# A hybrid state-space and attention layer: branch products over all tokens in three parts, an ungated first half, and fewer VectorE operations

## The chip, the core and the metric

The kernel runs on one core of a Trainium2 chip. The metric is the device time of one execution in microseconds (us); the kernel before takes 2579.67 us in the median of 3 runs (2579.16 to 2581.6). The core's engines run side by side, each through its own list of instructions in order: TensorE (PE; its weight loads are listed apart as PEld), VectorE (DVE), ScalarE (ACT), GpSimd (POOL) and SyncE (SP), which issues all DMAs of this kernel. Engines wait for one another by semaphores. Matrix products go to PSUM, everything else lies in SBUF, and large intermediate arrays go to scratch arrays in DRAM.

## The reference, cut to what matters

One layer is applied to 1024 tokens of a prompt and to 64 tokens of a running stream with caches. With xn = RMSNorm(x), one projection gives z, xBC, dt, q, k, v and two gates. Then:

```
proj = xn @ w_in
z, xbc, dt_raw, q, k, v, gate_ssm, gate_att = split(proj)
xbc_c = silu(causal_dwconv(xbc))                        # -> xs, bm, cm
y_ssm, ssm_new = ssd_scan(xs, softplus(dt_raw + bias), a_neg, bm, cm, ssm_past, 64)
y_ssm = group_rmsnorm((y_ssm + ssm_d * xs) * silu(z)) * ssm_norm_w
o = rmsnorm(diff_attention(rope(norm(q)), rope(norm(k)), v, lam)) * subln_w * (1 - lambda_init)
mix = sigmoid(gate_ssm) * (y_ssm @ w_branch_ssm) + sigmoid(gate_att) * (o @ w_branch_attn)
x = x + mix @ w_out
h = rmsnorm(x) @ w_up;  ha, hb = halves of h
x = x + (silu(causal_dwconv(ha)) * hb) @ w_down
```

`w_branch_ssm` has 2048 rows and 1024 columns, `w_branch_attn` and `w_out` 1024 by 1024. Everything is float32.

## The kernel before, in words

All activations lie transposed: 128 features on the partitions, the 1088 tokens (1024 + 64) along the free axis. `WIDE` cuts the tokens into 384, 384 and 320. Every large product is made in three passes for float32 accuracy: `weights` (line 125) loads a block of a weight matrix, rounds it into `w_hi` on ACT (line 136) and leaves the remainder `w_lo` on VectorE (line 137); `product` (line 140) issues hi*hi, hi*lo and lo*hi for each of 8 blocks of 128 rows, 24 matmuls into one PSUM tile. The pool `wp` has two sets of weight buffers; the PSUM pool `pm` has two tiles, handed out by `acc`.

The stages in order:

- Norm of the input in chunks of `NORM` tokens (lines 238 to 261). It writes `xn_hi` and `xn_lo`, two tiles of 8 x 1088 columns, on which all projections run. `rstd_of` (line 209) makes 1/sqrt(mean + eps) from a logarithm, an exponential and one Newton step, four VectorE operations.
- `values`, `heads` for q and k, `steps` for dt. `steps` also writes the running sums of dt*a to `a_sc` and their exponentials to `e_sc`, both in DRAM.
- Attention by heads (line 616). The remaining projections are a stream of tiles, `ORDER` (line 67): z, convolved xBC ("c") and gates ("g"), each block of 128 features in three parts of tokens. `fill(rate)` takes `rate` tiles of that stream after each piece of work, `ATT_STEPS` in attention and `SCAN_STEPS` in the scan. The gates are kept as tanh(g/2), so that sigmoid(g) is (1 + tanh)/2, and the half is put into the output projection (line 805).
- The scan, `scan` (line 731): 4 groups of heads by 3 spans of tokens, each span of three steps of 128 tokens (`step`, line 658) and a closing `gated` (line 714). A step loads running sums as `bc`, to all partitions (line 663), and their exponentials as `e2` (line 668); `bc` is masked on POOL (line 682), goes through eight exponentials on ACT (line 684) and a multiply on VectorE (line 685), and is the operand of the products `yi`. Products `ye` with the state are scaled by `e2` (line 697). `fetch` loads the next span, `gate` applies silu to it on ACT, with the change of the activation table that this needs. `gated` normalizes and writes `y_sc`.
- The branch products, `branch` (line 156), three times: the attention output (`o_sc`, with its gate, to `m_sc`), the first half of the scan's channels (`y_sc[:D]`, gate and `m_sc` added, to `n_sc`), the second half (`y_sc[D:]`, gate and `n_sc` added, split into `mix`). Tokens are cut into two halves of 544; for each half, 8 blocks of output rows; for each block the weights are loaded and split again, and two products of 272 columns made. VectorE empties PSUM with the gating multiply (line 196) and adds the earlier branch (line 198). Rows of `y_sc` come through staging tiles `b_f` (three buffers) and are split on ACT and VectorE (lines 167 to 170); rows of `o_sc` were stored split and are loaded directly. Their pool `br` takes the place of `xn_pool` after that is released.
- The first two branches are the tail of the stream: from scan span `BRANCH_AT` on, `fill` takes tiles of `branch_tiles` (line 756). What is left runs after the scan, then the third branch (line 784), then the output projection with the second norm (line 793) and the feed-forward part (line 826).

The order on each engine comes from a planner, not from the text alone: it walks a timeline of expected durations, and of the instructions that are then ready it takes those that stand first in the text, moved up by `tc.high_priority(ahead)`. A branch tile can therefore be issued earlier than its place in the text where TensorE would be free. `issue_after` pins an instruction behind another. Pools that are released and reallocated make the new tiles wait for the last use of the old ones.

Of the kernel before, what the change touches and what calls it, by code (L numbers as in the profile page):

```python
# [31 lines left out]
NORM = (128, 256, 256, 256, 192)  # L32
# [10 lines left out]
BG = 4  # L43
LAG = 2
# [13 lines left out]
SCAN_STEPS = 2.5  # L58
SPLIT = 5
BRANCH_AT = 9  # L60


def group(g):
# [4 lines left out]
         ("z", range(4, 8)), ("c", group(3)), ("z", range(8, 16)))  # L68
# [8 lines left out]
def hybrid_layer(ctx: ExitStack, tc: tile.TileContext, xT, prm, cst, rope, wvd, win, wbs, wba, wout, wup, wdn,  # L77
# [18 lines left out]
    a_sc, e_sc = scratch("a_sc", [32, T]), scratch("e_sc", [32, T])  # L96
# [24 lines left out]
    xn_hi = xn_pool.tile([P, KT, T], R32, name="xn_hi")  # L121
    xn_lo = xn_pool.tile([P, KT, T], R32, name="xn_lo")
# [24 lines left out]
    def project(block, evac):  # L147
        w_hi, w_lo = weights(block, KT, P)
        for c, w in WIDE:
            ps = acc(w)  # L150
            product(ps, [(w_hi[:, k], w_lo[:, k], xn_hi[:, k, c : c + w], xn_lo[:, k, c : c + w]) for k in range(KT)])
            with tc.high_priority(quick or ahead):
                evac(ps, c, w)
            yield

    def branch(stage, pair, src, wts, g0, add, out):
        def octet():
            return [br.tile([P, 8, HALF], R32, name=n, tag=n, bufs=2) for n in ("b_hi", "b_lo")]

        def bring(c, k, hi, lo):  # L160
            if stage is None:
                for u, t in enumerate((hi, lo)):
                    load(out=t[:, k].bitcast(F32), in_=src[D * u + P * k : D * u + P * (k + 1), c : c + HALF])
                return
            for a in (0, HALF // 2):
                q = slice(a, a + HALF // 2)
                t = stage()
                load(out=t, in_=src[P * k : P * (k + 1), c + a : c + a + HALF // 2])
                S.copy(hi[:, k, q], t)
                V.tensor_tensor(out=lo[:, k, q], in0=t, in1=hi[:, k, q], op=ALU.subtract)  # L170

        parts = [octet(), None]
        for k in range(8):
            bring(0, k, *parts[0])
        for x, c in enumerate((0, HALF)):
            hi, lo = parts[x]
            if x == 0:
                parts[1] = octet()
            for m in range(KT):
                r = slice(P * m, P * (m + 1))  # L180
                two = pair()
                gt, at = two[:, :HALF], two[:, HALF:T]
# [809 lines left out]
```

## Time and profile before

| what | value |
|---|---|
| median of 3 runs | 2579.67 us |
| profiled execution, its own time | 2582.58 us |
| span of that execution, first to last instruction | 2580.8 us |
| mean granted TensorE clock | 0.995 |
| TensorE idle time in the span | 55.8 us (2580.8 - 2525.0) |
| scan with projection tiles | 1097 to 1262 us |
| scan with branch products | 1262 to 1592 us |
| third branch | 1592 to 1691 us |
| output projection and second norm | 1691 to 1802 us |

A stretch of the span is described by one line of the window view: its borders and length in us, then for each engine the busy us and, in brackets, the number of instructions, then the granted TensorE clock (1.00 is full), the share of time in which the 16 DMA engines were busy, and GB/s. A line of the view of waits reads: engine and line that waited, what ended the wait, total us, number of times, longest. A line of the group view reads: line, engine, operation, output<-inputs, sizes, count | busy us, mean ns of one | idle us of the engine just before them, and what ended it. Matmuls overlap in the pipeline, so the spacing of their starts, not the duration listed, is what one costs.

### The profile page before, as it was taken

The numbers are of one execution on the slowest core, as the hardware profiler recorded it, in microseconds if no ns is written. First come the engines' busy times: TensorE is split into PE (matmuls) and PEld (weight loads), VectorE is DVE, ScalarE is ACT, GpSimd is POOL, SyncE is SP. The second block draws the span as 40 slices with busy tenths as digits, with TensorE's granted clock in tenths as the row PEclk, the third lists the DMA queues.
The fourth block names the chain that finished last, engine by engine and source line by source line (L and its number), as shares of the span: only waits on it lengthen the run. The fifth ranks groups of instructions, "written<-read, shape, count | busy, mean of one in ns | idle before, by whom it ended". The sixth has DMA issues, their size and how long they took to land.

```text
span 2580.8 us, 41810 instructions
## 1 busy us (share of the span) xinstructions
PE 2525.0 (98%) x16484; PEld 2444.8 (95%) x16484; DVE 1399.8 (54%) x2371; ACT 1032.2 (40%) x2113; POOL 290.0 (11%) x387
## 2 busy tenths in 40 slices
PE   8999999999999999999999989999999999999999
PEld 7999999999999999988788879999999999999999
DVE  7326266654447674665679997658333333343333
ACT  5334234544445554565456643335312222131221
POOL 3000001000001110022333430023000000000000
PEclk9999999999999999999999999999999999999999
DMA  5217167545435433176798978555311111111112
GB/s 162 83 54 282 51 257 213 153 142 148 131 126 164 136 112 111 64 232 192 245 332 258 304 246 272 195 187 193 119 42 47 44 42 50 42 50 40 44 43 77
DMA packets 233685, 366.59 MB, mean 142 GB/s; under 512 B 31184, under 2 KB 160464, under 8 KB 233360
## 3 DMA queue, kind: packets, MB, share of 16 engines
q1 hardware_dynamic: 233488, 363.91, 44.2%
q8 instruction: 130, 2.13, 0.3%
q14 instruction: 67, 0.55, 0.1%
HBM read 263.56 MB, written 100.27 MB: 141 GB/s over the span
## 4 chain that ended last, share of the span: by engine, by line
PE 43%; DMA 3%; DVE 3%; ACT 1%; issue 1%; SPq 0%; POOL 0%; DVEq 0%; ACTq 0%; POOLq 0%
PE mm L143 7%; PE mm L145 7%; PE mm L144 7%; PE up L143 7%; PE up L145 7%; PE up L144 7%; DMA in<-x_sc 1%; DMA b_hi<-o_sc 1%; DVE w_lo L137 1%; PE yi L689 1%; PE stp L702 0%; ACT bc L684 0%; DVE y L728 0%; DMA in<-z_sc 0%; DVE b_lo L170 0%
## 5 line engine op out<-in xcount | busy, mean ns | idle before, releaser
L143 PE MATMUL mm<-xn_hi,w_hi 128*128 128x320 f32 (+1 forms) x1496 | 497.9, 333 | 2.3 <-ACT zr L428 1.1
L145 PE MATMUL mm<-xn_hi,w_lo 128*128 128x320 f32 (+1 forms) x1496 | 496.8, 332 | 0.0
L144 PE MATMUL mm<-xn_lo,w_hi 128*128 128x320 f32 (+1 forms) x1496 | 494.6, 331 | 0.0
L136 ACT CAST w_hi<-w_f 128x1024 fp32r<-128x1024 f32 (+2 forms) x220 | 229.3, 1042 | 547.2 <-PE mm L144 369.3
L137 DVE TENSOR_TENSOR w_lo<-w_f,w_hi 128x1024 fp32r<-128x1024 f32 (+2 forms) x220 | 284.9, 1295 | 300.8 <-ACT w_hi L136 298.4
L143 PE MATMUL up<-x_hi,w_hi 128*128 128x384 f32 (+1 forms) x1056 | 345.0, 327 | 2.7 <-ACT x_hi L820 2.7
L144 PE MATMUL up<-x_lo,w_hi 128*128 128x384 f32 (+1 forms) x1056 | 344.8, 327 | 0.0
L145 PE MATMUL up<-x_hi,w_lo 128*128 128x384 f32 (+1 forms) x1056 | 343.3, 327 | 0.0
L143 PEld LDWEIGHTS mm<-xn_hi,w_hi 128*128 128x128 f32 x1496 | 281.9, 188 | 7.9 <-issue 2.8
L145 PEld LDWEIGHTS mm<-xn_hi,w_lo 128*128 128x128 f32 x1496 | 281.6, 188 | 2.9 <-issue 1.9
L144 PEld LDWEIGHTS mm<-xn_lo,w_hi 128*128 128x128 f32 x1496 | 281.8, 188 | 2.6 <-issue 1.3
L143 PE MATMUL mm<-b_hi,w_hi 128*128 128x272 f32 x768 | 228.0, 298 | 19.1 <-DVE b_g L196 15.9
L144 PE MATMUL mm<-b_lo,w_hi 128*128 128x272 f32 x768 | 227.2, 296 | 0.7 <-DMA b_lo<-o_sc 0.7
L145 PE MATMUL mm<-b_hi,w_lo 128*128 128x272 f32 x768 | 227.5, 297 | 0.0
L143 PEld LDWEIGHTS up<-x_hi,w_hi 128*128 128x128 f32 x1056 | 198.7, 188 | 3.1 <-ACT x_hi L820 3.0
L144 PEld LDWEIGHTS up<-x_lo,w_hi 128*128 128x128 f32 x1056 | 198.8, 188 | 0.1
L145 PEld LDWEIGHTS up<-x_hi,w_lo 128*128 128x128 f32 x1056 | 198.5, 188 | 0.0
L880 DVE TENSOR_TENSOR xa<-xa,mm 128x384 f32<-128x384 f32 x144 | 76.5, 531 | 197.3 <-PE mm L145 197.3
L144 PE MATMUL mm<-f_lo,w_hi 128*128 128x384 f32 (+1 forms) x528 | 173.1, 328 | 0.0
L143 PE MATMUL mm<-f_hi,w_hi 128*128 128x384 f32 (+1 forms) x528 | 173.0, 328 | 0.0
L145 PE MATMUL mm<-f_hi,w_lo 128*128 128x384 f32 (+1 forms) x528 | 173.0, 328 | 0.0
L143 PEld LDWEIGHTS mm<-b_hi,w_hi 128*128 128x128 f32 x768 | 147.3, 192 | 25.4 <-DVE b_g L196 15.4
(252 smaller groups left out, 4803.7 us busy)
## 6 DMA issues: line engine op xcount, KB each, us to landing
w_f<-in_win_dram SPq DMA_DIRECT2D x76, 512.0 KB, 4.0
w_f<-in_wup_dram SPq DMA_DIRECT2D x44, 512.0 KB, 3.7
bc<-a_sc SPq DMA_DIRECT2D x32, 512.0 KB, 6.3
w_f<-in_wbs_dram SPq DMA_DIRECT2D x32, 512.0 KB, 4.2
b_g<-g_sc SPq DMA_DIRECT2D x48, 272.0 KB, 4.5
w_f<-in_wout_dram SPq DMA_DIRECT2D x24, 512.0 KB, 3.8
x_sc<-cc SPq DMA_DIRECT2D x48, 192.0 KB, 1.9
kh_t<-k_st SPq DMA_DIRECT2D x32, 272.0 KB, 6.9
```

The costliest lines, as they stand in the source:

```text
L136: S.copy(hi, w)
L137: V.tensor_tensor(out=lo, in0=w, in1=hi, op=ALU.subtract)
L143: PE.matmul(ps, a_hi, b_hi, start=i == 0, stop=False)
L144: PE.matmul(ps, a_hi, b_lo, start=False, stop=False)
L145: PE.matmul(ps, a_lo, b_hi, start=False, stop=i == n - 1)
L689: PE.matmul(yi[u : u + 64, e // 2, :L], xdt[:L, e], bc[:L, e, :L], start=True, stop=True)
L880: V.tensor_tensor(out=xa[:, m, c : c + w], in0=xa[:, m, c : c + w], in1=ps, op=ALU.add)
```

## The change

- `branch` runs over all 1088 tokens: for a turn of one or two blocks of output rows (`TURNS`) it loads and splits the weights once and then makes products of 384, 384 and 320 columns for the three parts of `WIDE`. One call yields 24 tiles instead of 16 larger ones.
- Projection rows and branch rows are kept as three pairs of tiles, one per part of `WIDE`, and the branch rows use the same tags of `xn_pool`: each part takes the place of the earlier part as soon as that has had its last use. The last two z blocks run part by part in alternation.
- The second branch is stored without gate and sum (ACT copies it out of PSUM). The third branch adds it to its own product, gates the sum once, and adds the attention branch: three VectorE operations a tile.
- `SCAN_STEPS` 2.5 becomes 1.65 and `BRANCH_AT` 9 becomes 4; side tiles `b_g` become eight of 384 columns instead of four of 1088.
- The exponentials `e2` are made in the step by two ACT instructions from `bc`, ahead of the mask; `e_sc` goes.
- The two multiplies with dt in the step become one with a broadcast operand.
- `rstd_of` gives the negative root with one more ACT square and two VectorE operations instead of four; the norm weights in `par` are negated once to make up for it.
- `NORM` has six chunks instead of five, with borders on those of `WIDE`.

```diff
-NORM = (128, 256, 256, 256, 192)
+NORM = (128, 256, 192, 192, 192, 128)
-BG = 4
-LAG = 2
+BG = 8
+TURNS = ((0, 1), (2,), (3,), (4,), (5,), (6, 7))
-SCAN_STEPS = 2.5
+SCAN_STEPS = 1.65
-BRANCH_AT = 9
+BRANCH_AT = 4
-         ("z", range(4, 8)), ("c", group(3)), ("z", range(8, 16)))
+         ("z", range(4, 8)), ("c", group(3)), ("z", range(8, 14)))
+    def rows_by_part(name):
+        return [[xn_pool.tile([P, KT, w], R32, name=f"{name}_{u}{x}", tag=f"{u}{x}") for u in ("hi", "lo")]
+                for x, (c, w) in enumerate(WIDE)]
+    xn = rows_by_part("xn")
...
+    def branch(stage, side, src, wts, gates, adds, out):
+        parts = rows_by_part("b")
+        for (c, w), (hi, lo) in zip(WIDE, parts):
+            for k in range(8):
+                if stage is None:
+                    for u, t in enumerate((hi, lo)):
+                        load(out=t[:, k].bitcast(F32), in_=src[D * u + P * k : D * u + P * (k + 1), c : c + w])
+                else:
+                    t = stage()[:, :w]
+                    load(out=t, in_=src[P * k : P * (k + 1), c : c + w])
+                    S.copy(hi[:, k], t)
+                    V.tensor_tensor(out=lo[:, k], in0=t, in1=hi[:, k], op=ALU.subtract)
+        for ms in TURNS:
+            wt = [weights(wts[m], KT, P) for m in ms]
+            for (c, w), (hi, lo) in zip(WIDE, parts):
+                for m, (w_hi, w_lo) in zip(ms, wt):
+                    beside = []
+                    for d, r0 in ([(g_sc, gates)] if gates is not None else []) + [(d, 0) for d in adds]:
+                        t = side()[:, :w]
+                        load(out=t, in_=d[r0 + P * m : r0 + P * (m + 1), c : c + w])
+                        beside.append(t)
+                    to = beside[0] if beside else side()[:, :w]
+                    ps = acc(w)
+                    product(ps, [(w_hi[:, k], w_lo[:, k], hi[:, k], lo[:, k]) for k in range(KT)])
                     with tc.high_priority(ahead):
+                        if not beside:
+                            S.copy(to, ps)
+                        elif not adds:
+                            V.scalar_tensor_tensor(to, to, 1.0, ps, ALU.add, ALU.mult)
+                        else:
+                            V.tensor_tensor(out=beside[1], in0=beside[1], in1=ps, op=ALU.add)
+                    if adds:
+                        V.scalar_tensor_tensor(to, to, 1.0, beside[1], ALU.add, ALU.mult)
+                        V.tensor_tensor(out=to, in0=to, in1=beside[2], op=ALU.add)
+                    out(m, c, to)
+                    yield
...
         act(r, u, AF.Exp, scale=-0.5)
-        V.tensor_scalar(u, mean, -0.5 * scale, -0.5 * EPS, ALU.mult, ALU.add)
-        V.tensor_tensor(out=u, in0=u, in1=r, op=ALU.mult)
-        V.tensor_tensor(out=u, in0=u, in1=r, op=ALU.mult)
-        V.scalar_tensor_tensor(out, u, 1.5, r, ALU.add, ALU.mult)
+        act(u, r, AF.Square, scale=math.sqrt(0.5 * scale))
+        V.scalar_tensor_tensor(u, mean, EPS / scale, u, ALU.add, ALU.mult)
+        V.scalar_tensor_tensor(out, u, -1.5, r, ALU.add, ALU.mult)
...
+                for a, b in ((O_MIX, O_CW), (O_SN, O_D), (O_QN, O_FW)):
+                    V.tensor_scalar_mul(par[:, a:b], par[:, a:b], -1.0)
...
+        two = [z_tiles([j]) for j in (14, 15)]
+        for _ in WIDE:
+            for u in two:
+                yield next(u)
...
-            ev = e_sc.rearrange("(j u) t -> u j t", u=2)
             for u in range(2):
-                src = ev[u, 4 * g : 4 * g + 4, c0 : c0 + L].unsqueeze(0).to_broadcast([64, 4, L])
-                load(out=e2[64 * u : 64 * u + 64, :, :L], in_=src)
+                half = slice(64 * u, 64 * u + 64)
+                act(e2[half, :, :L], bc.rearrange("p (j u) t -> p u j t", u=2)[half, u, :, :L], AF.Exp)
...
-            for dst, sc in ((xdt, dt_tok), (xw, dtw)):
-                V.tensor_tensor(out=dst[:L], in0=tr3, in1=sc[:L, ch, h8].unsqueeze(2).to_broadcast([L, 8, 64]), op=ALU.mult)
+            V.tensor_tensor(out=xx[:L], in0=tr3, in1=dtt[:L, :, ch, h8].unsqueeze(3).to_broadcast([L, 2, 8, 64]), op=ALU.mult)
...
-            yield from branch(None, pair, o_sc, wba, D, None, store(m_sc))
-            yield from branch(stage, pair, y_sc[:D], wbs[0], 0, m_sc, store(n_sc))
+            yield from branch(None, side, o_sc, wba, D, (), store(m_sc))
+            yield from branch(stage, side, y_sc[:D], wbs[0], None, (), store(n_sc))
...
-    run(branch(stage, pair, y_sc[D:], wbs[1], 0, n_sc, mixed))
+    run(branch(stage, side, y_sc[D:], wbs[1], 0, (n_sc, m_sc), mixed))
```

90 lines of the change are left out of this document (23 added, 67 removed).

## The prediction

> **What bounds the kernel now.** I read the page's busy times first, then windows cut at stage borders (found in the trace as first and last instruction of a stage), then who waited for whom in the scan, then the VectorE groups there.
>
> ```profile
> PE 2525.0 (98%) x16484; PEld 2444.8 (95%) x16484; DVE 1399.8 (54%) x2371; ACT 1032.2 (40%) x2113; POOL 290.0 (11%) x387
> ```
>
> TensorE is the bound: of 2580.8 us it sits idle 55.8. So only three things pay: fewer or cheaper matmuls, idle time of TensorE, and a slowed clock. Where the idle time lies (scan with projection rows; scan with branch products; third branch; output projection):
>
> ```profile
> core 0: us, PE busy (x) PEld busy (x) DVE busy (x) ACT busy (x) POOL busy (x), PEclk, DMA share, GB/s
> 1097.00:1262.00 165.00, 156.49 (x1032) 143.13 (x1030) 88.51 (x126) 96.34 (x189) 47.95 (x41) 1.00 0.66 206
> 1262.00:1592.00 330.00, 303.82 (x2362) 272.29 (x2363) 289.99 (x414) 177.20 (x357) 119.89 (x74) 0.97 0.89 287
> 1592.00:1691.00 99.00, 99.00 (x789) 99.00 (x788) 58.79 (x96) 32.49 (x47) 0.00 (x0) 1.00 0.60 196
> 1691.00:1802.00 111.00, 107.81 (x641) 106.26 (x640) 77.23 (x104) 51.44 (x79) 34.19 (x23) 0.99 0.63 209
> ```
>
> 8.5 us idle in the first stretch (5%), 26.2 in the second (8%), where the granted clock is 0.97 too (330 x 0.03 = 9.9 us) and VectorE works 88% of the time. The slowed clock lies in short dips:
>
> ```profile
> 1300.00:1320.00 20.00, 17.40 (x123) 16.73 (x122) 14.14 (x17) 14.76 (x26) 7.28 (x5) 0.91 1.04 358
> 1380.00:1400.00 20.00, 15.41 (x104) 14.12 (x103) 15.07 (x21) 8.04 (x21) 4.32 (x3) 0.83 0.55 174
> 1520.00:1540.00 20.00, 15.59 (x109) 13.80 (x108) 19.88 (x25) 8.43 (x20) 8.30 (x4) 0.91 0.62 208
> ```
>
> Each stands where TensorE idles longest. What ends those waits (us in total, times, longest):
>
> ```profile
> PE mm L143 <- DVE b_g L196: 15.9, 8, 4.6
> PE tr L671 <- ACT in L653: 4.3, 5, 1.6
> POOL bc L682 <- DMA bc<-a_sc: 63.7, 21, 8.7
> ACT b_hi L169 <- DMA b_f<-y_sc: 24.6, 15, 4.1
> ```
>
> The largest wait of TensorE in the scan is a branch product that finds both PSUM tiles full, because VectorE has not yet done the gating multiply (line 196) that empties them. VectorE's load between 1097 and 1600 us:
>
> ```profile
> L137 DVE TENSOR_TENSOR w_lo<-w_f,w_hi 128x1024 fp32r<-128x1024 f32 x43 | 68.8, 1599 | 24.0 <-ACT w_hi L136 23.9
> L196 DVE SCALAR_TENSOR_TENSOR b_g<-b_g,mm 128x272 f32<-128x272 f32 x65 | 27.5, 426 | 12.6 <-PE mm L145 12.5
> L681 DVE TENSOR_TENSOR xw<-tr,dtw 128x512 f32<-128x512 f32 x32 | 21.7, 677 | 0.0
> L697 DVE TENSOR_TENSOR y<-ye,e 128x256 f32<-128x256 f32 x4 | 1.7, 416 | 3.0 <-PE ye L696 3.0
> L198 DVE TENSOR_TENSOR b_g<-b_g 128x544 f32<-128x544 f32 x16 | 12.9, 804 | 0.2
> L216 DVE TENSOR_TENSOR gn<-gn,gn 128x384 f32<-128x384 f32 x8 | 5.3, 662 | 0.1
> ```
>
> **The change, part by part.**
>
> *Shape of the branch products.* 3 branches x 8 row blocks x 96 matmuls of 272 columns become 72 of 384, 384 and 320: 2304 matmuls become 1728, columns unchanged. Two stretches without idle time give the price:
>
> ```profile
> 1613.00:1678.00 65.00, 65.00 (x519) 65.00 (x518) 39.87 (x64) 21.73 (x31) 0.00 (x0) 1.00 0.59 197
> 1871.00:1935.00 64.00, 64.00 (x388) 64.00 (x387) 22.43 (x35) 10.50 (x15) 1.32 (x4) 1.00 0.13 42
> ```
>
> The first holds 272-column products: 65/518 = 125.5 ns each, 12.05 us per row block. The second holds the 384/384/320 mix: 64/387 = 165.4 ns, 11.91 us. That is 0.14 x 24 = 3.4 us; by single starts in the timeline (125.7, 173.3 and 146.2 ns: 12.07 against 11.83) it is 5.8. I take **-4.5**. The Trainium skill, page "TensorE: Matmul & The Clock Gate", section "Back-to-back issue gap", gives a warm matmul columns/2.4 plus 2.5 ns, so by it 576 fewer would save an estimated 1.4 us; the rows show a larger fixed share per matmul, and the measurement decides.
>
> *VectorE work within the scan* (branches 1 and 2 lie there). Weights are split once per row block, not once per half: 16 fewer remainders at 1.22 (median) to 1.60 (mean), -20 us. The second branch is no longer gated or added to: 32 x 0.426 + 16 x 0.804 = -26.5. Two products with dt become one: 256 and 512 elements cost 0.416 and 0.68, so a fixed 0.15 each, 36 x 0.15 = -5. The reciprocal root loses two of four operations a span: 12 x about 1.2 = -14. Sum -65 of the 378 us that the two stretches show; over some 480 us that is 65% busy instead of 88% where it hurts. None of this is on the path itself; it counts only through the 15.9 us. I let a quarter of them stay: **-12** (ends -15.9 and -4). The third branch takes the displaced operations (three of about 0.5 us a tile, its own split 0.55 and a third of a weight split 0.4, about 2.5 us against a product of 3.96); VectorE stays the quicker one there.
>
> *Clock.* The page of windows shows four such dips in the scan, 20 x (0.09 + 0.17 + 0.09 + 0.09) = 8.8 us. They follow the waits: **-5** (0 to -8.8).
>
> *Rows into the place of the projection rows, part by part.* Now all rows wait until the last projection ends (b_hi and b_lo loads 1.9 us of TensorE wait, 16.09 of 20 us busy between 1260 and 1280). Afterwards the last two z blocks run interleaved, so the first part comes free 4 tiles earlier, 15 us of cover for loads landing in 6.9: **-2** (0 to -4). Its price: these loads stand in SP's queue until TensorE has let the part go, and the scan's own loads (bc, next span) stand behind them. SP gets relief: 72 loads of e at 0.586 us of its time, and 512 KB of weights 24 times, are gone. I cost it at nothing, covered by the three bc buffers; without that cover 6.
>
> *Staging of the second and third branch.* Rows come through three buffers: in the trace, casts come three at a time every 6 us (1559-1561, 1565, 1572-1574), so 24 chunks take 48 us. The cover is the last turn's other parts and the next turn's first two, about 15 + 17 us of products, plus the scan's own matmuls for branch 2. Part one is in time, the end of part three late by 0 to 8: **+3**.
>
> *Turns.* A pair of row blocks holds both weight buffers; the next block's split (1.04 + 1.22 us) must fit under the last product of the pair's second member, 3.5 us, where before it had 6. Three such places a branch, and ACT and VectorE have other work queued: **+3** (0 to +10).
>
> *Two exponentials a step instead of loads of e.* 72 of 64x512, between 0.39 (128 columns) and 0.585 (copy of 512): nearest is the latter, 42 us on ACT, plus 24 copies of 0.47 out of PSUM, 12 squares of 0.53, minus 16 casts of 1.04: ACT goes from 273 to about 315 of 480 us. Beside other work; zero on the path, and it puts 1.2 us into the chain load-select-exponential, which POOL's waits cover as long as TensorE has fill products. It is the fourth rival if not.
>
> *Norm chunks, signs, rstd elsewhere.* Three small negations once and 15 further short ACT and VectorE instructions against two VectorE operations fewer in each chunk, while VectorE is full (5.0 of 5.0 us from 20 to 50 us): **-1** (-2 to +1). The last root before the up projection exchanges operations of the same length: 0.
>
> **Sum**: -4.5 -12 -5 -2 +3 +3 -1 = -18.5. The profiled execution took 2582.6 (span 2580.8 and 1.8 around it), 2.9 over the median of the runs: 2582.6 - 18.5 = 2564.1, as a median **2561**.
>
> **Rivals.**
> 1. *As summed*: 2561; with its terms' ends 2546 to 2574.
> 2. *Even laying lifts the whole scan.* Idle and clock loss (34.7 + 9.9 us) fall to 12, since every engine gets cover: -33 -4.5 -2 = -39, 2541. For it: VectorE falls to 65% everywhere. Against: the first stretch has 5% idle although VectorE is at 54% there.
> 3. *The stall moves.* What VectorE gives back returns at the turns, the staging and the ACT copies: only shape and rows pay, and +6 takes it back: 2579. For it: 24.6 us of ACT waiting on rows.
> 4. *Slower: ACT is held by the bc load.* POOL waits 63.7 us for it now; the two exponentials take that wait to ACT, behind them stand weight casts, PSUM copies and the eight exponentials, and PSUM has two tiles, 4 us of cover. If half of the wait comes through, +32 on -18.5: 2593. It decides from 19 us on, 30% of the wait. Against: ACT is idle a third of the time, and the order is laid for the loads' expected landing. The same page of the Trainium skill, specification table, has ScalarE's queue as strict first in, first out, which is the rule behind this rival; no row before shows an ACT instruction overtaking another.
>
> **How the numbers follow.** Chances: 0.50, 0.22, 0.13, 0.15. The predicted time is the first's. Leaving out the fourth and the outer edges of the second, the range is 2536 to 2583. A measurement here tells 0.2% (5 us) from no change: faster means under 2574.5, slower over 2584.8. The first case and the second are nearly all faster, the third mostly same: faster 0.74, same 0.12, slower 0.14.
>
> **What would show it.** Right: branch matmuls 384 and 320 wide, 1728 of them; TensorE's wait on the gating multiply under 5 us; VectorE under 75% in the whole scan; one dip of the clock or two. Wrong: a wait of a product on a weight remainder or on late rows of 5 us or more at the start of the second or third branch (terms +3 and +3 too small); ACT waiting on the bc load by tens of us and TensorE on ACT copies (rival 4); the scan's idle share still 7% with VectorE at 65% (then VectorE was not the cause).

## The result

The changed kernel takes 2576.09 us in the median of 20 runs (2568.86 to 2581.92), the kernel before 2580.93 beside it (20 runs, 2578.1 to 2585.42). The ratio is 0.9979 with a 95% interval of 0.9972 to 0.9987: faster by 5.4 us, 0.21%. The sign is as forecast and the time lies in the range, but of 18.5 us that were summed, less than a third came. The profiled execution took 2576.3 us, 6.3 less than that of before. Two executions on record took two to three times as long as the others, one of the kernel before (8096 us) and one of a later kernel (5072 us); the ratios leave them out.

The page's busy times of the changed kernel:

```profile
span 2574.2 us, 40564 instructions
PE 2525.0 (98%) x15924; PEld 2440.6 (95%) x15924; DVE 1321.2 (51%) x2238; ACT 1074.9 (42%) x2219; POOL 288.3 (11%) x393
```

TensorE is busy as long as before, 2525.0 us, although it issues 560 fewer matmuls; the whole 6.6 us by which the span shrank are idle time, 49.2 instead of 55.8. VectorE lost 78.6 us of work and ScalarE gained 42.7; in the scan alone it is -72 and +44, where the working had -65 and +42. So two questions stand: why the idle time fell so little, and why fewer matmuls did not make TensorE's work shorter.

Windows of the changed kernel, cut at the stage borders of its trace: scan with projection rows, scan with branch products, third branch, output projection.

```profile
core 0: us, PE busy (x) PEld busy (x) DVE busy (x) ACT busy (x) POOL busy (x), PEclk, DMA share, GB/s
1097.00:1286.00 189.00, 180.09 (x1207) 161.16 (x1206) 124.94 (x159) 140.36 (x275) 67.40 (x56) 0.99 0.65 206
1286.00:1588.00 302.00, 285.79 (x1848) 256.86 (x1847) 186.11 (x248) 180.15 (x358) 96.87 (x62) 0.96 0.64 207
1588.00:1687.00 99.00, 96.66 (x580) 95.17 (x580) 65.09 (x119) 25.71 (x47) 0.00 (x0) 1.00 0.66 205
1687.00:1798.00 111.00, 109.07 (x650) 107.39 (x650) 74.74 (x103) 52.27 (x83) 32.44 (x23) 1.00 0.67 213
```

VectorE works 66% and 62% of the two scan stretches, where it worked 88% in the second. Idle time of TensorE is 8.9 and 16.2 us there (before: 8.5 and 26.2). The third branch, which had none, has 2.3 us, and the clock in the second stretch is 0.96. Length and idle time of every stage, with the same borders in both traces (first and last instruction of a stage):

| stage | length before | after | idle before | after |
|---|---|---|---|---|
| up to the first score | 410.0 | 408.6 | 9.6 | 8.6 |
| attention | 706.8 | 712.1 | 6.6 | 8.9 |
| scan | 477.7 | 467.2 | 33.1 | 23.6 |
| third branch | 96.6 | 99.0 | 0.0 | 2.3 |
| output projection | 97.1 | 97.3 | 0.5 | 0.6 |
| feed-forward | 792.6 | 790.0 | 6.0 | 5.1 |

The scan gave 10.5 us; attention and the third branch took some of it back, in places where the change was costed at -1 and +3. Of the feed-forward's 2.6 us, 0.9 are idle time and 1.7 a dip of the clock at 1800 us that is gone. What ended TensorE's waits in the changed kernel (whole span; us in total, times, longest; rows that the kernel before has at about the same size are left out):

```profile
PE mm L148 <- ACT b_g L188: 4.5, 1, 4.5
PE mm L148 <- ACT zr L429: 4.1, 4, 2.1
PE sc L543 <- ACT p_t L557: 3.8, 1, 3.8
PE ye L699 <- DMA state<-in_st_dram: 3.2, 2, 2.6
PE mm L150 <- DVE w_lo L142: 2.8, 3, 1.6
PE mm L148 <- DVE b_g L190: 2.8, 1, 2.8
PE mm L148 <- DVE b_g L192: 0.5, 1, 0.5
```

The gating wait, 15.9 us before, is 2.8 + 0.5 now. In its place stand other waits. Two are new: a branch product behind ScalarE's copy of a PSUM tile (line 188) and the state's load. Two have grown: projection rows behind ScalarE (line 429), 1.1 us before, and at the start of attention a score behind the exponential of line 557, 2.0 us before.

Four stretches of the changed kernel in which the granted clock dips:

```profile
1240.00:1260.00 20.00, 17.91 (x116) 16.23 (x115) 10.59 (x13) 13.42 (x22) 8.71 (x6) 0.91 0.40 105
1300.00:1320.00 20.00, 14.81 (x99) 12.40 (x98) 10.24 (x16) 10.56 (x18) 1.27 (x3) 0.83 0.99 334
1440.00:1460.00 20.00, 17.39 (x94) 14.48 (x95) 14.46 (x24) 17.28 (x35) 5.58 (x4) 0.74 0.85 287
1480.00:1500.00 20.00, 15.47 (x94) 14.11 (x94) 6.32 (x8) 18.01 (x31) 3.80 (x4) 0.83 0.39 129
```

They make 20 x (0.09 + 0.17 + 0.26 + 0.17) = 13.8 us against 8.8 before. Some of that falls into waits; in the clock's records of the scan the slowed time in which TensorE was busy grew from 15.7 to 23.1 us, which at half speed costs 3.7 us more (2.0 over the whole span, since the dip at 1800 us is gone). It is not one execution's chance: the mean granted clock over all runs on record is 0.9958 for the kernel before (91 runs) and 0.9941 for the changed one (32 runs), that is 11.0 and 15.2 us of lost clock, waits included. The 2.0 us in this trace, and 2.6 us more of busy time ahead of the scan, 16 small matmuls of the norm among it, are about what the new shape of the products saved (3 to 6 us, below); so the busy time did not move.

### The profile page after: what moved, and what is told of

Same layout as the page of the kernel before. It is cut to its first block, busy times and chain, and to the rows that moved or that the text cites. A ratio compares the mean times of both kernels' runs of the same rounds, so it can differ in the third digit from the quotient of the medians.

```text
span 2574.2 us, 40564 instructions
## 1 busy us (share of the span) xinstructions
PE 2525.0 (98%) x15924; PEld 2440.6 (95%) x15924; DVE 1321.2 (51%) x2238; ACT 1074.9 (42%) x2219; POOL 288.3 (11%) x393
## 4 chain that ended last, share of the span: by engine, by line
PE 47%; DMA 5%; ACT 2%; DVE 1%; issue 1%; SPq 0%; POOL 0%; DVEq 0%; ACTq 0%; POOLq 0%
PE mm L148 8%; PE mm L150 8%; PE mm L149 8%; PE up L148 7%; PE up L149 7%; PE up L150 7%; DMA bc<-a_sc 1%; PE yi L692 1%; DMA b_f<-y_sc 1%; PE stp L705 1%; PE ye L699 1%; DMA in<-x_sc 1%; ACT bc L687 0%; DVE w_lo L142 0%; DVE b_lo L173 0%
## 5 line engine op out<-in xcount | busy, mean ns | idle before, releaser
L142 DVE TENSOR_TENSOR w_lo<-w_f,w_hi 128x1024 fp32r<-128x1024 f32 (+2 forms) x196 | 247.9, 1265 | 301.4 <-ACT w_hi L141 298.7
L141 ACT CAST w_hi<-w_f 128x1024 fp32r<-128x1024 f32 (+2 forms) x196 | 203.9, 1041 | 458.9 <-PE mm L149 297.5
L148 PE MATMUL mm<-b_hi,w_hi 128*128 128x384 f32 (+1 forms) x576 | 196.4, 341 | 9.1 <-ACT b_g L188 4.5
L150 PE MATMUL mm<-b_hi,w_lo 128*128 128x384 f32 (+1 forms) x576 | 193.2, 336 | 2.2 <-DVE w_lo L142 2.2
L149 PE MATMUL mm<-b_lo,w_hi 128*128 128x384 f32 (+1 forms) x576 | 192.7, 335 | 0.0
L458 DVE SCALAR_TENSOR_TENSOR cc<-pre,par,cc 128x384 f32<-128x384 f32 (+1 forms) x216 | 128.4, 595 | 45.3 <-ACT cc L456 42.2
```

Source lines behind the costliest of these rows:

```text
L141: S.copy(hi, w)
L142: V.tensor_tensor(out=lo, in0=w, in1=hi, op=ALU.subtract)
L148: PE.matmul(ps, a_hi, b_hi, start=i == 0, stop=False)
L149: PE.matmul(ps, a_hi, b_lo, start=False, stop=False)
L150: PE.matmul(ps, a_lo, b_hi, start=False, stop=i == n - 1)
L458: V.scalar_tensor_tensor(cc[:, :m], pre[:, i : i + m], cw(i), cc[:, :m], ALU.mult, ALU.add)
```

## The experiments

My theory behind the trace: the change does what it says to VectorE, and gives most of it back through three of its own parts that were costed near nothing: the exponentials `e2` ("e" in short) on ScalarE, the short root at the start of attention, and the three-buffer staging of rows. Rivals: VectorE was never the cause and something else holds the scan; the even laying itself (how the stream's tiles are spread over the scan, by `SCAN_STEPS` and `BRANCH_AT`) costs; the rows' loads block SP's queue. Each kernel computes the whole result. All ratios are to the kernel before, measured beside it; the changed kernel itself stands at 0.9979 and, repeated, at 0.9974 (middle 0.9977).

| kernel | median us (runs) | ratio, 95% |
|---|---|---|
| the change, repeated | 2575.09 (12) | 0.9974 (0.9964 to 0.9983) |
| silu of a step in one piece | 2572.51 (11) | 0.9968 (0.9955 to 0.998) |
| e loaded again | 2570.15 (12) | 0.9962 (0.9951 to 0.9974) |
| old root for q and k heads | 2571.88 (11) | 0.9964 (0.9951 to 0.9977) |
| five staging buffers | 2570.21 (8) | 0.9955 (0.9938 to 0.9972) |
| the last three together | 2563.54 (6) | 0.9932 (0.9914 to 0.995) |
| before, with VectorE's economies alone | 2583.16 (12) | 1.0006 (0.9992 to 1.002) |
| the change without VectorE's economies and exponentials | 2572.78 (11) | 0.9967 (0.9953 to 0.9981) |
| other laying | 2576.61 (12) | 0.9986 (0.9973 to 0.9999) |
| rows in 12 loads, not 48 | 2576.78 (12) | 0.9983 (0.9973 to 0.9994) |
| three together, rows in 12 loads | 2566.42 (6) | 0.994 (0.9928 to 0.9952) |
| three together, rows' loads held back | 2567.22 (6) | 0.9946 (0.9932 to 0.9961) |

### The change, repeated

> The changed kernel itself once more, on the chip of the two others. Its order of instructions is the same, so the waits of TensorE recur by name within 1 us each (copy of the second branch 4.5, projection copies 4.1, state load 3.2). If the dips of the clock belong to the waits, they lie within 10 us of 424, 1247, 1309, 1445 and 1490 us and sum to 14 us give or take 4; if they are chance, they lie elsewhere. Time 2570 to 2582, ratio 0.997 to 0.999.

2575.09 us. The waits are the same again: copy of line 188 3.9 us, line 429 5.5 (1.4 more, not within 1 us), state 3.9, gating multiply 2.8. The clock dips at 424, 1311, 1448 and 1492 us, where it dipped at 425, 1309, 1445 and 1490; these belong to the program. The fifth dip, at 1247 us, is not there; one stands at 1219 us instead, so its place is chance in part. The last section shows what decides it.

### The exponentials of e: taken off ScalarE

ScalarE's timeline of the changed kernel (start us, us, engine, line, op) around the largest new wait:

```profile
1479.57 1.28 ACT L658 ACT_TABLE_LOAD   x1 [4.68 <-DMA in<-x_sc]
1480.86 1.81 ACT L658 ACTIVATE in<-in 128x1920 f32<-128x1920 f32 x1
1482.68 1.28 ACT L672 ACT_TABLE_LOAD   x1
1483.98 1.27 ACT L672 ACTIVATE e<-bc 64x512 f32<-64x512 f32 x2
1485.27 1.28 ACT L658 ACT_TABLE_LOAD   x1
1486.57 1.80 ACT L658 ACTIVATE in<-in 128x1920 f32<-128x1920 f32 x1
1488.39 1.28 ACT L660 ACT_TABLE_LOAD   x1
1489.68 1.04 ACT L141 CAST w_hi<-w_f 128x1024 fp32r<-128x1024 f32 x1
1490.63 0.42 ACT L188 COPY b_g<-mm 128x320 f32<-128x320 f32 x1
```

and TensorE's there:

```profile
1491.10 0.69 PE L148 MATMUL mm<-b_hi,w_hi 128*128 128x384 f32 x1 [4.53 <-ACT b_g L188]
```

The two exponentials of a step were planned between the two halves of the silu, at this one place of the scan. They need another activation table, so the pair costs 1.27 us and two loads of 1.28, and the copy that empties TensorE's PSUM tile stands last in the row, behind all of it. The sum had counted 42 us of exponentials (they are 43.6) and no table loads. The Trainium skill's page "ScalarE: Activation LUTs", section "What ACT_TABLE_LOAD costs", gives 1283 ns for the load, which these rows show; its further 1380 ns of drain they don't: the exponential starts 1.30 us after the load does.

First test, the exponentials away, e loaded from DRAM as before:

```
-                act(e2[half, :, :L], bc.rearrange("p (j u) t -> p u j t", u=2)[half, u, :, :L], AF.Exp)
+                src = ev[u, 4 * g : 4 * g + 4, c0 : c0 + L].unsqueeze(0).to_broadcast([64, 4, L])
+                load(out=e2[64 * u : 64 * u + 64, :, :L], in_=src)
```

> The changed kernel with e loaded from DRAM again, as before; all else of the change stays. Theory A: ScalarE does 44 us less in the scan, the mask on GpSimd waits for the load alone, TensorE's idle time in the scan falls from 25 us to 18 or less, time 3 to 8 us below the changed kernel (ratio 0.9948 to 0.9967). Theory B: idle 22 to 28 us, time within 2 us of the changed kernel. A third way: SyncE's queue, 42 us fuller, delays other loads and the time rises by 2 to 5 us.

0.9962, some 4 us (0.0015 of 2581) under the change. The wait on line 188's copy shrinks to 1.0 us, and the scan is 460.9 us instead of 467.2. Its idle time is nearly the same (22.8 us against 23.6, where theory A had 7 us less), with a new largest wait:

```profile
PE yi L695 <- DVE bc L691: 5.9, 2, 5.6
```

What fell is the slowed clock: by its records the scan lost 8.5 us to it in this trace, and 13.7 in the change. Over all runs the granted clock accounts for 2 of the 4 us at most (13.3 us lost against 15.2).

Second test, the table loads away and the exponentials kept: the silu is one instruction, so nothing fits between its halves.

```
-SPLIT = 5
+SPLIT = 10
```

> The changed kernel with silu of a span as one instruction instead of two halves, so that nothing can come between the halves. Theory A (the work put on ScalarE took over the wait: exponentials of e between the halves cost two more table loads each time, and PSUM copies stand behind them): table loads in the scan fall from 28 to 24, the 4.5 us wait of TensorE on the copy of the second branch goes, the time falls by 2 to 6 us against the changed kernel (ratio to the kernel before 0.9955 to 0.997). Theory B (the rest of the gain went into dips of the clock and waits that fall anew in every order): within 2 us of the changed kernel, whatever the table loads do.

Table loads of the scan with this kernel's lines:

```profile
L658 ACT ACT_TABLE_LOAD x12 | 15.4, 1283 | 54.1 <-DMA in<-z_sc 54.1
L660 ACT ACT_TABLE_LOAD x12 | 15.4, 1283 | 0.2
```

Four fewer than in the changed kernel, where lines 658, 660, 672 and 687 have 14, 12, 1 and 1. The wait on line 188 is gone and the scan takes 454.2 us, 13 less. But attention and the third branch are 6.5 and 3.9 longer in this trace (its third branch idles 4.6 us), and the ratio gains only 0.0009, 2.3 us, which its interval does not tell from the change. Both tests take the wait away; that the table loads between the halves made it, and not the exponentials' 1.27 us, is what the timeline shows at this place, and its price of 2 to 4 us is at the edge of what the runs can tell.

### The short root and the start of attention

Windows of the first 30 us from the first score on, in the kernel before:

```profile
410.00:440.00 30.00, 27.17 (x160) 25.83 (x160) 17.63 (x38) 11.86 (x27) 1.38 (x9) 0.94 0.89 245
```

in the changed kernel:

```profile
408.60:438.60 30.00, 24.91 (x137) 23.01 (x136) 15.99 (x35) 11.46 (x25) 3.29 (x7) 0.94 0.95 237
```

and in the changed kernel with the old root for the q and k heads alone:

```profile
411.30:441.30 30.00, 25.64 (x148) 23.97 (x147) 15.91 (x31) 10.90 (x23) 1.28 (x8) 0.94 0.92 244
```

The edit:

```
+        if tag == "qn":
+            V.tensor_scalar(u, mean, -0.5 * scale, -0.5 * EPS, ALU.mult, ALU.add)
+            V.tensor_tensor(out=u, in0=u, in1=r, op=ALU.mult)
+            V.tensor_tensor(out=u, in0=u, in1=r, op=ALU.mult)
+            V.scalar_tensor_tensor(out, u, 1.5, r, ALU.add, ALU.mult)
+            return
         act(u, r, AF.Square, scale=math.sqrt(0.5 * scale))
```

> The changed kernel with the old root of four VectorE operations for the q and k heads alone (their weights positive again). In four kernels with the short root attention's last score starts 4 to 9 us later than in the kernel before (1072.9 us) with the same projection tiles done, 3672 matmuls. Theory R (the short root makes the planner put the first scores ahead of projection tiles, while their rows are still landing): the first score finds 927 projection matmuls issued, not 910, the 4 us wait of TensorE near 420 us goes, the last score starts at 1071 to 1074, and the time is 3 to 6 us below the changed kernel. Rival (the loss comes from elsewhere in the norm or from chance): the last score stays at 1076 or later and the time within 2 us.

0.9964, 3.4 us under the change. With the short root the planner lets the first score start when 910 projection matmuls have been issued, with the old one 927; a score 16 us later then waits on the exponential for 3.8 us with no projection product ahead of it. I had expected this wait to go with the old root. It did not: it stands 10 us later and takes 3.0 us (2.0 before), and TensorE idles 4.4 of the first 30 us instead of 5.1 (2.8 before). The last score came later than I expected, at 1075.8 us against 1076.8 in the change, so this pair of traces shows 1 us of the 3.4. One trace is thin for this; here are all of them: with the short root, TensorE idles 7.1 to 9.6 us between first and last score in eight kernels (the change 7.4), and with the old one 4.5 to 6.4 us in six. The groups don't overlap. Their last scores, for the same matmuls up to there but for 16 small ones, stand at 1077.9 us on the mean of the seven changed kernels with the short root and at 1073.8 for the old. So the short root does cost some 3 to 4 us up to the end of attention; by which wait is not shown.

### VectorE's economies without the branches, and the branches without them

The kernel before, with the short root and one product with dt:

```
-        V.tensor_scalar(u, mean, -0.5 * scale, -0.5 * EPS, ALU.mult, ALU.add)
-        V.tensor_tensor(out=u, in0=u, in1=r, op=ALU.mult)
-        V.tensor_tensor(out=u, in0=u, in1=r, op=ALU.mult)
-        V.scalar_tensor_tensor(out, u, 1.5, r, ALU.add, ALU.mult)
+        act(u, r, AF.Square, scale=math.sqrt(0.5 * scale))
+        V.scalar_tensor_tensor(u, mean, EPS / scale, u, ALU.add, ALU.mult)
+        V.scalar_tensor_tensor(out, u, -1.5, r, ALU.add, ALU.mult)
...
-            for dst, sc in ((xdt, dt_tok), (xw, dtw)):
-                V.tensor_tensor(out=dst[:L], in0=tr3, in1=sc[:L, ch, h8].unsqueeze(2).to_broadcast([L, 8, 64]), op=ALU.mult)
+            V.tensor_tensor(out=xx[:L], in0=tr3, in1=dtt[:L, :, ch, h8].unsqueeze(3).to_broadcast([L, 2, 8, 64]), op=ALU.mult)
```

> The kernel before with two parts alone: the shorter reciprocal root (with the sign in the weights) and the one multiply with dt. About 19 us less VectorE work in the scan, 6 us more on ScalarE. If VectorE's load was the cause of the 15.9 us of TensorE's wait on the gating multiply, that wait falls by a third or more and the time by 4 to 9 us (ratio 0.9965 to 0.9985). If the wait comes from the order and not from the load, it stays within 3 us and the time within 2 us of the kernel before.

No change (1.0006). The waits of TensorE in its scan:

```profile
PE mm L143 <- DVE b_g L196: 10.7, 3, 6.2
PE yi L691 <- DVE xx L683: 3.9, 1, 3.9
```

Less work on VectorE shortened the gating wait from 15.9 to 10.7 us, a third as expected, the scan's idle time from 33.1 to 28.8 us and the scan by 6.9 us, although a new wait of 3.9 us appeared. So in this trace the economies do pay where they were meant to. Attention became 7.6 us longer, with the short root there, and the third branch 2.6 us, and that took it back.

The other way round: the change with e loaded, the old root everywhere and two products with dt.

```
-            load(out=a_sc, in_=af)
+            load(out=a_sc, in_=af)
+            load(out=e_sc, in_=ef)
...
-            V.tensor_tensor(out=xx[:L], in0=tr3, in1=dtt[:L, :, ch, h8].unsqueeze(3).to_broadcast([L, 2, 8, 64]), op=ALU.mult)
+            for dst, sc in ((xdt, dt_tok), (xw, dtw)):
+                V.tensor_tensor(out=dst[:L], in0=tr3, in1=sc[:L, ch, h8].unsqueeze(2).to_broadcast([L, 8, 64]), op=ALU.mult)
```

> The changed kernel without its VectorE economies outside the branches: old root everywhere, two multiplies with dt, e from DRAM; what stays is the branch products over all tokens, the places by part, the laying, the ungated second branch and the norm chunks. If the economies paid, it is slower than the kernel with e from DRAM (2570.2 us) by 5 us or more, with waits on the gating multiply back at 6 us or more. If they paid nothing, it lies within 3 us of it or below, and attention ends 3 to 5 us earlier.

0.9967: not slower than the change. The gating wait stays at 0.7 us, so the new branches alone remove it; the scan takes 462.9 us, 2 more than with the economies and e loaded (460.9), and attention is quicker (last score at 1071.3). Its largest wait is that of the kernel with e loaded, longer:

```profile
PE yi L695 <- DVE bc L691: 9.2, 3, 8.3
```

So in this kernel the economies shorten what VectorE does, and the whole, short root included, gains about nothing by them: against the change with e loaded the difference is 0.0005, under what these runs resolve. Going by single effects (0.9977 - 0.0015 - 0.0013) this kernel should have stood at 0.9949; the missing 0.0018, 4.6 us, would be the worth of the other economies, with an interval that reaches to nothing.

### Staging with five buffers

```
-BF = 3
+BF = 5
```

> The changed kernel with five staging tiles for branch rows instead of three. The third branch took 99.0 us against 96.6 before, 2.3 us of it idle, where the work itself is 1.2 us less. If staging is the cause, its idle time falls below 1 us, the stage to 96 to 97 us and the time by 2 to 3 us. If the weight splits at the turn are the cause, the idle time stays at 2 us.

0.9955, 5.7 us under the change. The third branch in this kernel:

```profile
1579.00:1676.00 97.00, 96.48 (x581) 95.22 (x580) 66.24 (x117) 26.31 (x46) 2.66 (x2) 1.00 0.66 206
```

Its idle time is 0.5 us instead of 2.3, as expected. The rest of the gain lies elsewhere: from the first product of one branch to that of the next, the first branch takes 147.6 us instead of 151.0 and the second 146.5 instead of 150.4. The first branch's own rows pass through no staging tile, so part of the 5.7 us is another order of the plan and not staging; how much, these runs don't tell. The third branch, where staging was the question, gave 2.1 us.

### The laying

```
-SCAN_STEPS = 1.65
+SCAN_STEPS = 2.5
-BRANCH_AT = 4
+BRANCH_AT = 9
```

> The changed kernel with the old laying: rate 2.5 and branch tiles from span 9 on. If even laying is what took the waits on the gating multiply away, they come back (10 us or more), idle time in the scan 33 us or more and the time 5 to 10 us above the changed kernel (ratio 0.9998 to 1.002). If the planner brings the branch tiles forward anyway, the branch products start within 15 us of where they started in the changed kernel (1286 us) and the time stays within 3 us.

0.9986, an interval that overlaps the change's. The branch products did not come later but 24 us earlier (first at 1262.8 us): the planner takes what is ready where nothing else is. In time, this says only that another laying is worth 0 to 2 us. In the trace it says more. The scan with the old laying, and its largest wait:

```profile
1121.20:1590.60 469.40, 437.68 (x2918) 389.58 (x2918) 291.68 (x377) 310.35 (x614) 169.05 (x107) 0.99 0.64 205
PE tr L675 <- ACT in L658: 15.1, 8, 4.3
```

VectorE is busy 62% of the scan (63% in the change), and no gating wait is left; yet TensorE idles 31.7 us, nearly as long as in the kernel before (33.1). The waits stand at the silu on ScalarE instead. With the new laying it idles 23.6. That the scan is only 2.2 us longer here than in the change comes from the clock, slowed for 10.2 us here and for 27.3 there. So in the changed kernel VectorE's relief took away the gating wait but little idle time, and the new laying took 8 us more.

### The three undone together

This kernel loads e, has the old root for the q and k heads, and five staging buffers.

> The changed kernel with e from DRAM, the old root for the q and k heads and five staging tiles. If the three causes add up: 6 us for e, 4 for the root, 2 for the staging, 2564 us (ratio 0.993 to 0.995). If each order of the plan brings its own stalls and dips, nothing over the kernel with e from DRAM alone: 2568 to 2572.

2563.54 us, 0.9932 (0.9914 to 0.995): 17.5 us faster than before, 11.6 us under the change, where the single effects make 3.9 + 3.4 + 5.7 = 13. It beats both kernels. Its interval is clear of the change's, which those of the single edits touch or overlap. The time is as expected, though of other parts (6, 4 and 2 us had been put down). Windows of its scan and third branch:

```profile
1097.00:1576.00 479.00, 456.85 (x3047) 409.57 (x3046) 311.20 (x405) 271.15 (x554) 158.88 (x116) 0.99 0.75 231
1576.00:1674.00 98.00, 97.29 (x583) 95.69 (x582) 66.64 (x118) 26.77 (x47) 2.65 (x2) 1.00 0.66 204
```

The scan idles 22.1 us (25.1 in the change, same cut) at a clock of 0.99: one dip is left instead of four. Over its six runs the granted clock loses 10.3 us, 4.9 less than in the change, so up to 5 of the 11.6 us come by way of the clock. Its largest wait, and the stretch where that lies:

```profile
PE yi L701 <- DVE bc L697: 7.1, 2, 5.9
```

```profile
1300.00:1320.00 20.00, 11.85 (x77) 10.57 (x77) 8.00 (x14) 8.77 (x14) 0.82 (x2) 0.74 1.02 338
```

### The loss at the start of the first branch

TensorE is busy 14.81 of the 20 us from 1300 to 1320 in the change and 11.85 in the best kernel, with the DMA engines full (0.99 and 1.02): here the rows of the first branch come into the place of the projection rows, in 48 loads. Is it SP's queue? Rows in loads of four blocks:

```
-                        load(out=t[:, k].bitcast(F32), in_=src[D * u + P * k : D * u + P * (k + 1), c : c + w])
+                        if k % 4 == 0:
+                            load(out=t[:, k : k + 4].bitcast(F32),
+                                 in_=src[D * u + P * k : D * u + P * (k + 4), c : c + w].rearrange("(j p) t -> p j t", p=P))
```

> The changed kernel with the attention rows of the first branch loaded four blocks at a time, 12 DMAs instead of 48, same bytes. Theory Q (these 48 issues fill SyncE's queue for 20 us, and the running sums and side tiles of the scan are issued behind them): TensorE's busy time between 1300 and 1320 us rises from 14.8 to 18 or more, and the time falls by 3 to 8 us against the changed kernel. Rival (the DMA engines are full there, share 1.0, whatever the queue does): busy time stays under 16 us and the time within 2 us.

0.9983: no gain, and 14.84 of 20 us busy there. The same edit on the best kernel:

> The kernel with e from DRAM, the old root for q and k and five staging tiles, and the rows four blocks at a time. In that kernel TensorE is busy 2.8 of 10 us from 1300 to 1310, waiting 6 us for a step whose running sums were issued at 1301.6, behind 24 row loads. Theory Q: that wait falls under 2 us, 12.3 us of idle time in the first branch to 7 or less, time 2555 to 2559. Rival: within 2 us of 2563.5.

0.994, no gain either. The wait for the step's running sums is indeed gone there, but in the same stretch the silu's input (4.2 us) and the state's load (3.2 us) are waited for instead, and the first branch idles 13.3 us. The number of loads in SP's queue is not the cause of the loss. Is it that all parts load at once? In the best kernel, the rows of parts two and three now wait until the first product of the part before is stored:

```
+                    if stage is None and m == 0 and c < 768:
+                        with tc.issue_after(done.ins):
+                            rows(c // 384 + 1)
```

> The kernel with e from DRAM, the old root for q and k and five staging tiles, with the attention rows of the second and third part loaded only after the first product of the part before them is stored. If the 9 MB burst of rows on full DMA engines (share 1.0 from 1270 to 1330 us) makes the scan's running sums, side tiles and next span late, TensorE's busy time from 1300 to 1320 us rises from 11.9 of 20 to 17 or more, idle time in the first branch falls from 12.3 us to 7 or less, and the time is 2556 to 2560 us. If products then wait for their rows instead, or the engines stay full all the same, it lies within 2 us of 2563.5 or above.

Windows of this kernel there and behind it:

```profile
1300.00:1320.00 20.00, 18.86 (x109) 14.03 (x108) 9.76 (x17) 7.17 (x7) 1.04 (x1) 0.92 1.03 361
1320.00:1330.00 10.00, 7.76 (x27) 5.99 (x26) 7.88 (x8) 4.84 (x12) 5.54 (x3) 0.50 0.99 315
```

Busy time came back as expected (18.86 of 20), and no time with it: the ratio is 0.9946, the next 10 us run at half clock, and the first branch is 156.7 us long instead of 154.4: it idles 7.3 us instead of 12.3, but the scan's clock is slow for 20.5 us instead of 10.2. The DMA share stays at 1. That full DMA engines delay whatever the scan loads in these 60 us would fit all three runs, but no run takes that load away, so the cause of this loss stays open.

## Why the prediction was right and wrong

*Bound, sign.* Right: TensorE is the bound, and idle time and clock decide. The gain was 5.4 us and not 18.5; rival 3, "the stall moves" (2579), describes the trace better than the forecast's first case, and its time is nearer.

*Where the missing 13 us are.* The steps that failed are the clock's term (-5 forecast, a loss of 3.7 in the scan measured) and the price of the norm and the short root (-1 forecast; attention and what stands ahead of it are 3.9 us longer, of which the run with the old root gives back 3.4). Together these two are 13.6 us. The scan's idle time itself fell by 9.5 us, about what VectorE (-12), rows (-2) and the scan's share of staging and turns add up to. The third branch is 2.4 us longer, and the feed-forward part, by luck, 2.6 shorter, 1.7 of it a dip that no term had.

*Shape, -4.5.* Right. 1728 branch matmuls; in the third branch, where no wait falls (1640 to 1680 us), starts are 173.7 ns apart at 384 columns and 146.2 at 320, against 125.8 at 272: per row block 48 x 0.1737 + 24 x 0.1462 = 11.85 against 12.08 us, 5.5 us in all. Over the whole third branch, with the slower starts behind its waits, it is 174.9 and 148.7 ns, and 2.7 us.

*VectorE's relief, -12.* The work went as summed, and the gating wait with it, below 5 us. The size came out, the step behind it did not: "a quarter stays" let TensorE's idle time follow the gating wait by VectorE's load alone, and the sum had no term for the laying. With the old laying, VectorE at 62% and the gating wait gone, the scan still idles 31.7 of 469.4 us, 7%, which is the sign of being wrong that the prediction had named; the silu's 15.1 us stand in the wait's place. A third of the relief in the kernel before, without exponentials on ScalarE, did lower the idle time by 4.3 us; so the load counts, but not by way of this one wait. That the new laying then brought the idle time to 23.6 us is luck for this term. What the wait was worth was set by what came next: ScalarE's copies, the state's load, the silu, the decay product bc.

*Clock, -5.* Wrong in sign, the largest miss: 3.7 us lost in the trace, by the windows of the four stretches even 5, and up to 4.3 over all runs. "They follow the waits" took the dips as going down with the total of the waits, and "each stands where TensorE idles longest" was a misreading: from 1260 to 1280 us the kernel before idles 3.9 us, longer than in two of the four dips, at full clock (last section). The scan's waits became shorter in total, but single ones of 1.8 to 4.5 us are left, and the scan has four dips where one or two were to be the sign of being right.

*Rows by part, -2.* TensorE's wait for the rows' loads, 1.9 us before, is gone as forecast. But the stretch in which they load, costed at nothing with 6 as the price without cover, loses 5.2 us of 20 at a clock of 0.83 (before, 3.9 us at full clock). The number of loads in SP's queue, which I had named, is not the cause.

*Staging, +3.* Too small by the run: five buffers instead of three bring 5.7 us, of which the third branch shows 2.1 and part of the rest is another order. I had worked out 48 us for the casts against 32 of cover and then let only the end of the third part be late.

*Turns, +3.* About right: in the branches 2.2 us of waits on weight remainders (1.6 and 0.6) and 0.7 on a rounded weight.

*Exponentials, 0.* They cost about 4 us. Rival 4 had the place right, the copies and casts behind the exponentials, but not the size: where TensorE waited longest, 4.5 us, two table loads and the exponentials stood ahead of the copy, and the whole is an eighth of rival 4's 32 us. ScalarE did wait in front of the exponentials, as rival 4 has it, 34.4 us in the scan:

```profile
L672 ACT ACTIVATE e<-bc 64x512 f32<-64x512 f32 (+1 forms) x72 | 43.6, 606 | 34.4 <-DVE y L700 17.7 <-DMA bc<-a_sc 13.1 <-DVE y L701 3.1
```

Only 13.1 us of that are the load of bc; most of the rest is for VectorE to free one of the two buffers of e, which the prediction had not listed. The Trainium skill's page "TensorE: Matmul & The Clock Gate", specification table, has ScalarE's queue as strictly in order. That agrees with the timeline from 1479 to 1491 us, where a copy of 0.42 us runs after 11 us of work planned ahead of it.

*Norm chunks and root, -1.* Wrong in sign at one place: the two operations fewer changed where the planner let attention begin, and that cost 3.4 us by the run; no duration of an instruction would have shown it.

*Range.* The ends of the terms as the prediction lists them add up to 2543 and 2591 us, not to 2546 and 2574; the measured time lies between the first two and 2 us above the last.

With e, the root and the staging set right, 17.5 us came in. That this is near 18.5 does not confirm the sum term by term: up to 5 us of it are clock, which the three edits were not made for.

## What to carry to other kernels

Where several engines are near their limit in turn, taking work off the one that ends the largest wait gains only up to the next one's lateness: list what ends second before pricing the first. Price the clock by the single waits of about 2 us and more, not by the total of all waits, and count with chance in where they fall. Price an instruction moved to ScalarE with its table loads at the place where it will stand, and with the PSUM copies behind it, not by its own duration. And a kernel whose order is planned from durations changes its order when any of them changes: shorter work ahead of a stage can start that stage with less cover.

## What was not expected of the hardware

The half-speed clock comes in pieces of 3.41 us (3.41, 6.83 and 10.24 in the clock's records), and three of the scan's four dips follow waits of TensorE that are shorter than that: 0.9 and 2.1 us before the dip at 1247 us, 1.8 before 1309, and 2.6 before the longest, 10.24 us from 1445 on. The Trainium skill's page "TensorE: Matmul & The Clock Gate", section "What's actually happening", has the clock fall after at least one idle window of some 3.4 us; if that means a window without any work, waits of 2 us would be harmless. These records don't bear that reading out. If the wait of 2.6 us set off the dip behind it, it cost up to 5 us more in clock; no run takes that wait alone away.

What they do show is a grid. In each of the 14 traces all half-speed records start a whole number of steps of 3.413 us apart. Cut along that grid (from 30 us on), 48 windows at full clock have TensorE idle for 1.9 us or more, and half speed follows all 48; it follows none of 10101 with less than 0.9 us idle, and 20 of 149 in between. So a wait of 2 us is dear when it falls into one window, and can be free when the grid cuts it in two. In the change the wait of 2.1 us at 1246 us lies in one window, and the dip at 1247 follows; in the repeat the same wait is cut, no window there idles more than 1.4 us, and the dip is missing. In the kernel before, this stretch idles 3.9 us, at most 1.6 of them in one window:

```profile
1260.00:1280.00 20.00, 16.09 (x131) 12.65 (x130) 15.45 (x22) 8.63 (x25) 5.40 (x5) 1.00 1.00 314
```

A matmul's start-to-start time over 272, 320 and 384 columns was 125.8, 146.5 and 174.8 ns on the two stretches without idle time in the kernel before (from 1613 and from 1871 us). Between 272 and 384 columns that is 0.438 ns a column, and a line through the two leaves 7 ns for no columns; 320 lies on it within 1 ns. That small share is all that a wider shape saved here.
